# A two-layer encoder on one core: two groups of small products spread over four quadrants of TensorE, new durations in a list schedule, and two groups of loads on another queue

## The chip, the cores and the metric
The kernel runs on one core of a Trainium2 chip. The core has TensorE (PE in the rows, PEld for its weight loads), VectorE (DVE), ScalarE (ACT), GpSimd (POOL) and SyncE (SP), which here only issues transfers. The metric is the device time of one execution in microseconds. The kernel before took 4117.68 us, the median of three runs (4116.34 to 4122.85).

## The reference
The input x is 1024 positions of 1024 columns in float32. Two layers run one after the other, and each does this:

```
u  = x @ w_in                              # one input projection, cut into the columns of three branches
A  = rwkv7(u_A) * silu(z_A)                # 16 heads of 64, forwards and backwards over the positions
        state = state*w + (state@(-kk)) b^T + v k^T ;  y = state @ r
B  = pool(u_B) * silu(z_B)                 # means over windows 2, 4, 8, 16, minus itself, times a matrix
C  = attention(u_C) * silu(z_C)            # rotary positions, three (window, dilation) groups
m  = sum over branches of sigmoid(gate) * (branch @ proj)
x  = LayerNorm(alpha * x + m @ w_out)
```

All matrices that carry the model are float32, and the result is float32.

## The kernel before, in words
Dense products are made from split numbers: a float32 weight tile is cast to a rounded high part (ScalarE, L551), its low part is the difference (GpSimd or VectorE, L552), and each product is three matmuls of 128x128 by 128x512: L583 (high by high), L584 (low by high) and L585 (high by low). Such three are called a triple here. The class `Dense` issues them and prepares a weight piece one piece ahead.

A layer has five stages. In the rwkv stage (0 to some 1220 us in layer 0) the recurrence is done in chunks of 64 positions: per chunk a 64x64 triangular system per head is inverted in steps (`T`, `U`, `X`, with products at L1054 and casts at L1059), v's right sides are multiplied by the inverse (`av`, L1022, copied from PSUM to SBUF by ScalarE at L1025), the product for the state update follows (`nkt`, L1008, copied at L1012), and then each chunk goes through four steps in order: `A` multiplies the state by the chunk's rows (L1143 and L1146; VectorE adds at L1150), `W` scales the state (ScalarE, L1154), `B` multiplies the right sides by the inverse (L1161; ScalarE copies the result to `uv` at L1165), and `Cc` makes the outputs and the new state from them (L1175, L1180; VectorE, L1185). A step treats two heads and two directions at once, so `B` is four 64x64 products and `A` eight; `av` treats four chunks of each direction together, 16 products. A 64x64 product takes one quadrant of TensorE's array, which the halves of rows and columns (`HS[h]`) name; in float32 it is two matmul instructions. In the attention stage (1240 to 1600 us) VectorE rotates q and k in three operations (L1387, L1391, L1394), and the score products (L1447) need the result. The pool stage follows (to 1760 us), then the projections of branches C and B (to 1860 us: `ev_c`, L1741, and `ev_b`, L1752 and L1754, take the dense results off PSUM; meanwhile branch A's gated output is read back, L1772, cast to its high part by ScalarE, L1776, and split by GpSimd, L1778), and last the merge (to 2056 us: projection of A, output weights `wor` L1819, product L1842 to L1844, normalisation L1870 to L1883).

The order on every engine is set by the class `Sched`. Pieces of work, `Th`, say which engines they use and for how long (`("P", 230.0)` is 230 ns on TensorE; D, A, G, S are VectorE, ScalarE, GpSimd and SP), what they need and give, and which ring of PSUM buffers they hold ("m" for side work, two slots; "d" for dense). At each turn the list takes the piece that can start earliest by these numbers, and fills TensorE with dense triples in between. Each engine then runs its own instructions in that order; a waiting instruction stops those behind it on its engine.

Of the kernel before, what the change touches and what calls it, by code (L numbers as in the profile page):

```python
# [10 lines left out]
F32 = mybir.dt.float32  # L11
# [371 lines left out]
def trunk(ctx: ExitStack, tc: tile.TileContext, a: dict, out, dbg=None):  # L383
# [124 lines left out]
    class Dense:  # L508
# [56 lines left out]
        def make(self, src, nk, rhs, evac, halves=(0, 1), needs=(), gives=(), ev=(("A", 570.0),), key=None, ering=(), first=False):  # L565
# [62 lines left out]
    def rwkv(l):  # L628
        P = pc["P"]
        w_in = a["w_in"][l]  # L630
        with ExitStack() as es:
# [136 lines left out]
            def pair_kk(j):  # L768
# [76 lines left out]
                o.append(Th(f5, [("G", 3770.0)]))  # L845
# [151 lines left out]
            def joint(j, q):  # L997
# [28 lines left out]
                return ([Th(nkt, [("P", 930.0), ("A", 500.0), ("A", 500.0)], needs=[("sc", d, Q) for d in range(2)], ring=("m", "m"), gives=[("nkt", Q)])],  # L1026
                        [Th(av, [("P", 930.0), ("A", 500.0)], needs=[("nt", Q), ("uv" if q in (1, 2) else "uv0", j)], ring=("m",), gives=[("av", Q)])])
# [95 lines left out]
            def seq(j, q):  # L1123
# [4 lines left out]
                def step(i):  # L1128
# [6 lines left out]
                    def A():  # L1135
# [831 lines left out]
```

## Time and profile before

| | |
|---|---|
| median of three runs | 4117.68 us (4116.34 to 4122.85) |
| profiled execution | 4110.03 us, of which the span of the trace 4107.9 us |
| granted clock of TensorE, mean | 0.990 of full speed |
| TensorE (matmul) busy | 3933.5 us, 96% of the span |
| VectorE | 2344.7 us, 57% |
| ScalarE | 2224.0 us, 54% |
| GpSimd | 1653.9 us, 40% |

The span of the trace is the time from the first to the last instruction; the time of the execution has 2.1 us around it. A busy share is an average over stages with different loads; the rows below are read stage by stage. A bracket behind a row is the idle time of the engine ahead of it and what ended that.

### The profile page before, as it was taken

To read this page: it belongs to the slowest core of one execution; us is meant where nothing else is said; L and a number is where in the kernel's file an instruction comes from. 1 tells how busy PE (TensorE), PEld (TensorE's weight loads), DVE (VectorE), ACT (ScalarE), POOL (GpSimd) and SP (SyncE) were. 2 spreads that over 40 slices of the span, in tenths; PEclk is the share of its full clock that TensorE was granted. 3 is DMA by queue.
4 is the path that set the end of the run, shared out by engine and by line. 5 is a ranking of instruction groups with operands and counts; after the bars stand their busy time and mean duration, and the time that the engine had idled before them with its cause. 6 is when DMAs were issued, how large, how long until landed. Compare 5 with 4: busy or idle time off the path is not lost. (4 is left out here: it accounts for less than half of the span.)

```text
span 4107.9 us, 120670 instructions
## 1 busy us (share of the span) xinstructions
PE 3933.5 (96%) x51576; PEld 3060.1 (74%) x51576; DVE 2344.7 (57%) x4233; ACT 2224.0 (54%) x4390; POOL 1653.9 (40%) x2498
## 2 busy tenths in 40 slices
PE   8999999999999999999989999999999999999998
PEld 6677777777777788877767777777777777888777
DVE  3776766665533554545647667766665245454456
ACT  5677787777643442322146777777677434433210
POOL 4343444344433343453233444454434334334532
PEclk9999999999999999999999999999999999999999
DMA  2111111111114442155311111111111244421653
GB/s 90 32 48 43 44 42 45 45 42 44 58 58 119 130 134 91 54 181 192 123 51 30 48 40 44 42 48 40 43 47 54 76 114 133 127 83 55 191 182 116
DMA packets 329192, 326.41 MB, mean 79 GB/s; under 512 B 23536, under 2 KB 264384, under 8 KB 328655
## 3 DMA queue, kind: packets, MB, share of 16 engines
q1 hardware_dynamic: 301551, 233.66, 19.1%
q0 software_dynamic: 27104, 85.04, 5.9%
q8 instruction: 404, 6.62, 0.7%
q14 instruction: 133, 1.09, 0.1%
HBM read 224.86 MB, written 81.99 MB: 75 GB/s over the span
## 5 line engine op out<-in xcount | busy, mean ns | idle before, releaser
L583 PE MATMUL psdn<-xh,wh 128*128 128x512 f32 x3136 | 1331.1, 424 | 9.1 <-ACT wh L551 8.2
L585 PE MATMUL psdn<-xh,wl 128*128 128x512 f32 x3136 | 1240.8, 396 | 9.5 <-POOL wl L552 9.3
L584 PE MATMUL psdn<-xl,wh 128*128 128x512 f32 x3136 | 1236.5, 394 | 0.0
L552 POOL TENSOR_TENSOR wl<-wr,wh 128x512 fp32r<-128x512 f32 (+1 forms) x436 | 599.4, 1375 | 1313.1 <-ACT wh L551 1287.5
L583 PEld LDWEIGHTS psdn<-xh,wh 128*128 128x128 f32 x3136 | 594.5, 190 | 169.0 <-issue 31.0
L585 PEld LDWEIGHTS psdn<-xh,wl 128*128 128x128 f32 x3136 | 593.8, 189 | 151.4 <-POOL wl L552 19.5
L584 PEld LDWEIGHTS psdn<-xl,wh 128*128 128x128 f32 x3136 | 596.2, 190 | 101.0 <-issue 4.8
L551 ACT CAST wh<-wr 128x512 fp32r<-128x512 f32 (+2 forms) x484 | 290.3, 600 | 697.6 <-PE psdn L584 351.1
L1059 ACT CAST U<-pst 64x512 f16<-64x512 f32 x768 | 444.8, 579 | 116.9 <-PE pst L1054 100.1
L1087 DVE TENSOR_TENSOR X<-pst,c 128x512 f16<-128x512 f32 x320 | 219.4, 685 | 198.2 <-PE pst L1054 198.1
L1185 DVE SCALAR_TENSOR_TENSOR sbd<-sqp,wc,sbd 128x64 f32<-128x64 f32 x480 | 113.8, 278 | 216.9 <-PE sqp L1180 156.4
L1165 ACT COPY uv<-sqp 64x128 f32<-64x128 f32 x512 | 131.5, 257 | 85.0 <-PE sqp L1161 76.9
L1054 PEld LDWEIGHTS <-X 64*64 64x64 f16 x6144 | 144.1, 108 | 26.6 <-DVE sc L983 8.4
L1154 ACT ACTIVATE sbd<-sbd,wc 128x64 f32<-128x64 f32 x480 | 140.3, 340 | 43.1 <-PE sqp L1146 30.6
L1071 POOL TENSOR_TENSOR nl<-sc,nh 64x512 f16<-64x512 f32 x128 | 154.7, 1209 | 8.2 <-ACT nh L1068 3.0
L1054 PE MATMUL pst<-U,X 64*64 64x64 f16 x5120 | 153.6, 197 | 2.1 <-ACT U L1059 0.9
L1161 PEld LDWEIGHTS sqp<-u,sc 64*64 64x64 f32 x2048 | 80.1, 133 | 91.4 <-issue 50.2
L978 PE MATMUL pssc<-ar,nk 64*64 64x128 f32 x4096 | 146.4, 274 | 0.4
L1054 PEld LDWEIGHTS <-U 64*64 64x64 f16 x5120 | 113.1, 109 | 44.9 <-issue 14.5
L1054 PE MATMUL pst<-X,U 64*64 64x64 f16 x5120 | 140.3, 194 | 0.3
L1143 PEld LDWEIGHTS sqp<-sbd,ar 64*64 64x64 f32 x2048 | 83.6, 133 | 73.9 <-issue 43.7
L1150 DVE TENSOR_TENSOR u<-sqp,sc 128x128 f32<-128x128 f32 x256 | 73.4, 287 | 113.5 <-PE sqp L1146 61.0
(707 smaller groups left out, 7707.5 us busy)
## 6 DMA issues: line engine op xcount, KB each, us to landing
wr<-in_w_in_dram SPq DMA_DIRECT2D x360, 256.0 KB, 2.9
sga<-gt POOLq DMA_DIRECT2D x96, 256.0 KB, 2.3
g<-sga SPq DMA_DIRECT2D x96, 256.0 KB, 4.4
wr<-in_proj_a_dram SPq DMA_DIRECT2D x64, 256.0 KB, 3.0
sza<-sz POOLq DMA_DIRECT2D x32, 256.0 KB, 3.2
bva<-bv POOLq DMA_DIRECT2D x32, 256.0 KB, 2.5
oa<-o POOLq DMA_DIRECT2D x32, 256.0 KB, 3.0
oat<-oa SPq DMA_DIRECT2D x32, 256.0 KB, 3.6
```

Source lines behind the costliest of these rows:

```text
L551: nc.scalar.copy(hi[:, 0:n, :], r[:, 0:n, :])
L552: self.lo.tensor_tensor(out=lo[:, 0:n, :], in0=r[:, 0:n, :], in1=hi[:, 0:n, :], op=ALU.subtract)
L583: nc.tensor.matmul(ps, lhsT=hi[:, kk, :], rhs=ah, start=(k == 0), stop=False)
L584: nc.tensor.matmul(ps, lhsT=hi[:, kk, :], rhs=al, start=False, stop=False)
L585: nc.tensor.matmul(ps, lhsT=lo[:, kk, :], rhs=ah, start=False, stop=(k == nk - 1))
L978: nc.tensor.matmul(ps[h][HS[h if x == 0 else 1 - h], c, :], lhsT=nk[HS[h], c, x, :], rhs=ar[HS[h], c].rearrange("p a t -> p (a t)"), start ...
L1054: nc.tensor.matmul(ps[HS[1 - h if mir else h], d, c], lhsT=l, rhs=r, start=start and d == 0 and c == 0, stop=stop, skip_group_check=True)
L1059: nc.scalar.copy(dst[HS[h]], ps[HS[1 - h]])
L1071: nc.gpsimd.tensor_tensor(out=nl[HS[h]], in0=sc[HS[h], :, :, h, 0:64], in1=nh[HS[h]], op=ALU.subtract)
L1087: tt(out=x, in0=ps[0], in1=mask(i + 1), op=ALU.mult)
L1154: act(sbd[d], sbd[d], AF.Copy, scale=J["wc", d, Q % NB][:, pl[d][0]:pl[d][0] + 1])
L1165: nc.scalar.copy(uv[HS[h], two, h, :], pu[HS[h], 128:256].rearrange("p (s e) -> p s e", s=2))
```

## The change
It has four parts. In `av` the 32 instructions go to four quadrants of two PSUM tiles instead of two quadrants of one; the first direction's half is copied whole and the second's in two halves of the partitions, since two of its quadrants are the other way round; it holds both slots of ring "m" (one after its first copy). In `B` the eight instructions go to four quadrants, those of one row half in one of the step's two PSUM tiles and those of the other in the other, with four copies of 64x64 instead of two of 64x128; in `A` the rows for `py` are issued ahead of those for `pu`. The durations that the list uses are other numbers in many places (of which two stand in the diff; TensorE's own durations elsewhere stay). Branch A's read-back and the output weights are issued on SP instead of GpSimd. The first read-back waits for VectorE's last product of the pool branch, y times its gate, L1692 before and L1696 now.

```diff
-                    sc, ps = J["sc", Q], psm.tile([128, 2, 4, 64], F32, tag="m", name="psav")
+                    sc = J["sc", Q]
+                    ps = [psm.tile([128, 4, 64], F32, tag="m", name="psav") for _ in range(2)]
                     uv = J["uv", j, int(q in (1, 2))]
-                    for d in range(2):
-                        for i in range(4):
+                    for i in range(4):
+                        for d in range(2):
                             c, n, _ = place(d, q, i)
                             for h in range(2):
-                                nc.tensor.matmul(ps[HS[h], d, i], lhsT=sc[HS[1 - h], d, c, h, 0:64], rhs=uv[HS[1 - h], n, h, :],
+                                nc.tensor.matmul(ps[d][HS[h if d == 0 else 1 - h], i], lhsT=sc[HS[1 - h], d, c, h, 0:64], rhs=uv[HS[1 - h], n, h, :],
                                                  start=True, stop=True, skip_group_check=True)
                     yield
-                    nc.scalar.copy(sc[:, :, :, 1, 0:64], ps)
+                    nc.scalar.copy(sc[:, 0, :, 1, 0:64], ps[0])
+                    yield "first"
+                    for h in range(2):
+                        nc.scalar.copy(sc[HS[h], 1, :, 1, 0:64], ps[1][HS[1 - h]])
                 return ([Th(nkt, [("P", 930.0), ("A", 500.0), ("A", 500.0)], needs=[("sc", d, Q) for d in range(2)], ring=("m", "m"), gives=[("nkt", Q)])],
-                        [Th(av, [("P", 930.0), ("A", 500.0)], needs=[("nt", Q), ("uv" if q in (1, 2) else "uv0", j)], ring=("m",), gives=[("av", Q)])])
+                        [Th(av, [("P", 480.0), ("A", 280.0), ("A", 560.0)], needs=[("nt", Q), ("uv" if q in (1, 2) else "uv0", j)], ring=("m", "m"), gives=[("av", Q)])])
...
+                                nc.tensor.matmul(py[HS[1 - h], y0 + 64 * s:y0 + 64 * s + 64], lhsT=ar[HS[h], c, 1, :], rhs=sbd[d][HS[h]],
+                                                 start=d == 0, stop=False, skip_group_check=True)
+                            for h in range(2):
                                 nc.tensor.matmul(pu[HS[h], 64 * d:64 * d + 64], lhsT=ar[HS[h], c, 0, :], rhs=sbd[d][HS[h]],
                                                  start=d == 0, stop=True, skip_group_check=True)
-                            for h in range(2):
-                                nc.tensor.matmul(py[HS[1 - h], y0 + 64 * s:y0 + 64 * s + 64], lhsT=ar[HS[h], c, 1, :], rhs=sbd[d][HS[h]],
-                                                 start=d == 0, stop=False, skip_group_check=True)
...
-                        pu, uv = J["p"][1], J["uv", j, io]
+                        p, uv = J["p"][::-1], J["uv", j, io]
                         for d in range(2):
-                            c, n, s = pl[d]
                             for h in range(2):
-                                nc.tensor.matmul(pu[HS[h], 128 + 64 * s:192 + 64 * s], lhsT=J["sc", Q][HS[h], d, c, 0, 0:64], rhs=J["u0"][HS[h], d, :],
+                                nc.tensor.matmul(p[h][HS[d], 384:448], lhsT=J["sc", Q][HS[h], d, pl[d][0], 0, 0:64], rhs=J["u0"][HS[h], d, :],
                                                  start=False, stop=True, skip_group_check=True)
                         yield
                         for h in range(2):
-                            nc.scalar.copy(uv[HS[h], two, h, :], pu[HS[h], 128:256].rearrange("p (s e) -> p s e", s=2))
+                            for d in range(2):
+                                nc.scalar.copy(uv[HS[h], pl[d][1], h, :], p[h][HS[d], 384:448])
...
-                    return [Th(A, [("P", 230.0), ("D", 220.0)], needs=na, gives=[("read", j, n)]), Th(B, [("P", 240.0), ("A", 400.0)]),
+                    return [Th(A, [("P", 230.0), ("D", 220.0)], needs=na, gives=[("read", j, n)]), Th(B, [("P", 130.0), ("A", 780.0)]),
...
-                                       side=(("A", 307.0), ("G" if self.lo is nc.gpsimd else "D", 620.0 if self.lo is nc.gpsimd else 335.0)) if kk == 0 and h == halves[0] else (),
+                                       side=(("A", 520.0), ("G" if self.lo is nc.gpsimd else "D", 1235.0 if self.lo is nc.gpsimd else 602.0)) if kk == 0 and h == halves[0] else (),
...
-                    o += [Th(f0, [("S", 3000.0)], needs=[("raw", n, ct)]), Th(f1, [("D", 1160.0)]), Th(f2, [("D", 1160.0)]),
-                          Th(f3, [("D", 1160.0)], gives=[("rope", n, ct)])]
+                    o += [Th(f0, [("S", 3000.0)], needs=[("raw", n, ct)]), Th(f1, [("D", 1900.0)]), Th(f2, [("D", 2070.0)]),
+                          Th(f3, [("D", 1500.0)], gives=[("rope", n, ct)])]
...
-                    nc.gpsimd.dma_start(out=t, in_=oz[k * 128:(k + 1) * 128, hs])
+                    nc.sync.dma_start(out=t, in_=oz[k * 128:(k + 1) * 128, hs])
...
-                load.append(Th(fn, [("G", 1040.0)], lag=LDW, needs=[("oas", l, n - 6)] if n > 5 else (), gives=[("oal", l, n)], chain=False))
+                load.append(Th(fn, [("S", 100.0)], lag=LDW, needs=[("oas", l, n - 6)] if n > 5 else (), gives=[("oal", l, n)], chain=False))
...
-                    nc.gpsimd.dma_start(out=t, in_=a["w_out"][l][k * 128:(k + 1) * 128, :])
+                    nc.sync.dma_start(out=t, in_=a["w_out"][l][k * 128:(k + 1) * 128, :])
...
-                return [Th(load, [("G", 1040.0)], lag=3500.0, needs=[("pa", 0)] + ([("wo", k - 3)] if k > 2 else []), gives=[("wl", k)], chain=False)], \
+                return [Th(load, [("S", 100.0)], lag=3500.0, needs=[("pa", 0)] + ([("wo", k - 3)] if k > 2 else []), gives=[("wl", k)], chain=False)], \
```

How it moves instructions. On TensorE at the start of the rwkv stage, the difference of the orders ahead of the first product L823 (`psr`, which needs the normed `nx`), with + for what stands there now; psdn is the dense result, and these are the last three of four triples that are put there:

```order
+L583 MATMUL psdn<-xh,wh 128x512
+L584 MATMUL psdn<-xl,wh 128x512
+L585 MATMUL psdn<-xh,wl 128x512
+L583 MATMUL psdn<-xh,wh 128x512
+L584 MATMUL psdn<-xl,wh 128x512
+L585 MATMUL psdn<-xh,wl 128x512
+L583 MATMUL psdn<-xh,wh 128x512
+L584 MATMUL psdn<-xl,wh 128x512
+L585 MATMUL psdn<-xh,wl 128x512
 L823 MATMUL psr<-cst,nx 128x128 x4
```

The first product L823 thus has eight triples behind the second L781 instead of four; the same count holds in layer 1. In the attention of either layer, counted in dense triples of the whole program up to the product, the six products L1447 (L1451 now) that open an attention unit stand 4, 4, 4, 1, 4 and 1 triples later. The last L1246 of the rwkv stage has 18 triples between itself and the last `Cc` instead of 14.

On ScalarE at the head of the projections, before (y is the pool branch, wr a weight piece as loaded and wh its cast, ozt branch A's output as read back and xh its cast):

```order
L1689 ACTIVATE y<-psdn,pc 128x512 x2
L551 CAST wh<-wr 128x512
L551 CAST wh<-wr 128x256 x2
L1776 CAST xh<-ozt 128x512 x2
L551 CAST wh<-wr 128x512
L1776 CAST xh<-ozt 128x512
```

And the same place now:

```order
L1693 ACTIVATE y<-psdn,pc 128x512 x2
L1780 CAST xh<-ozt 128x512
L551 CAST wh<-wr 128x512
L1780 CAST xh<-ozt 128x512 x2
L551 CAST wh<-wr 128x256
L1780 CAST xh<-ozt 128x512 x3
L551 CAST wh<-wr 128x256
```

One cast of the read-back now stands between the last work on the pool branch and the cast of a weight piece of 128x512, and the casts of weights have one to three of them ahead of each.

On GpSimd at the same place, before (obl is the low part of the pool branch, m and t the sums of the projections, xl the low part of the read-back):

```order
L1694 TENSOR_TENSOR obl<-y,obh 128x512 x2
L1772 DMA ozt<-oz 128x512 x6
L1754 TENSOR_TENSOR m<-m,t 128x512
L1778 TENSOR_TENSOR xl<-ozt,xh 128x512
L1754 TENSOR_TENSOR m<-m,t 128x512
L1772 DMA ozt<-oz 128x512
L1778 TENSOR_TENSOR xl<-ozt,xh 128x512 x2
L1772 DMA ozt<-oz 128x512 x2
L1778 TENSOR_TENSOR xl<-ozt,xh 128x512 x2
```

And now:

```order
L1698 TENSOR_TENSOR obl<-y,obh 128x512 x2
L1782 TENSOR_TENSOR xl<-ozt,xh 128x512 x6
L1758 TENSOR_TENSOR m<-m,t 128x512 x2
L1782 TENSOR_TENSOR xl<-ozt,xh 128x512 x6
L1758 TENSOR_TENSOR m<-m,t 128x512 x2
L1782 TENSOR_TENSOR xl<-ozt,xh 128x512 x4
```

The loads of ozt are gone from this engine, and its subtractions for branch A stand in runs of six, six and four, with the sums of the projections between them.

## Rows read from the trace of the kernel before

**Rows 1.** Busy time of each engine in four stretches (columns in the first line).
```profile
core 0: us, PE busy (x) PEld busy (x) DVE busy (x) ACT busy (x) POOL busy (x), PEclk, DMA share, GB/s
200.00:1200.00 1000.00, 979.74 (x19863) 735.62 (x19858) 641.34 (x1345) 739.75 (x1537) 423.97 (x800) 1.00 0.15 46
...
1240.00:1600.00 360.00, 347.31 (x1872) 286.34 (x1871) 175.59 (x272) 141.96 (x264) 134.80 (x135) 0.99 0.43 125
1760.00:1860.00 100.00, 91.62 (x384) 72.61 (x383) 47.45 (x58) 20.14 (x40) 53.35 (x50) 0.98 0.63 200
1860.00:2056.00 196.00, 187.10 (x820) 148.69 (x820) 122.61 (x202) 37.59 (x61) 61.59 (x50) 0.98 0.47 155
```

**Rows 2.** TensorE's waits over the span: total us, times, longest us.
```profile
PE pssc L1447 <- DVE rawk L1394: 25.5, 12, 3.0
PE psdn L583 <- DVE m L1741: 16.3, 6, 5.2
PE sqp L1161 <- DVE u L1150: 14.4, 31, 1.7
PE psr L823 <- ACT nx L796: 12.1, 4, 5.9
PE psy L1246 <- POOL ysq L1241: 10.6, 8, 4.1
...
PE sqp L1175 <- ACT uv L1165: 0.7, 2, 0.4
```

**Rows 3.** Timeline: start us, length us, line, operation, count: a step's B.
```profile
439.18 0.45 PE L1161 MATMUL sqp<-u,sc 64*64 64x64 f32 x8
...
439.56 0.50 PE L583 MATMUL psdn<-xh,wh 128*128 128x512 f32 x1
```

**Rows 4.** Timeline: the inverse's product and the dense matmul behind it.
```profile
833.15 1.15 PE L1022 MATMUL psav<-uv,sc 64*64 64x64 f32 x32
...
834.23 0.51 PE L583 MATMUL psdn<-xh,wh 128*128 128x512 f32 x1
```

**Rows 5.** Timeline: the state update's product on four quadrants.
```profile
455.89 1.11 PE L1008 MATMUL psnt<-cst,nk 64*64 64x64 f32 x64
...
456.93 0.50 PE L583 MATMUL psdn<-xh,wh 128*128 128x512 f32 x1
```

**Rows 6.** ScalarE's copies by line: count, ns minimum, median and maximum.
```profile
L1165 ACT COPY uv<-sqp x512: 240/260/263, 157.7 to 3248.8; 64x128 f32<-64x128 f32 x171
...
L1025 ACT COPY sc<-psav x64: 562/586/598, 128.8 to 3209.8; 128x512 f32<-128x512 f32 x64
```

**Rows 7.** Timeline: first and last score product of layer 0, idle time in brackets.
```profile
1263.61 0.95 PE L1447 MATMUL pssc<-rawk,rawq 64*128 64x128 f32 x6 [2.95 <-DVE rawk L1394]
...
1508.83 0.49 PE L1447 MATMUL pssc<-rawk,rawq 64*128 64x256 f32 x2 [0.75 <-DVE rawk L1394]
```

**Rows 8.** Timeline: the head of the projections, layer 0.
```profile
1759.22 0.61 ACT L551 CAST wh<-wr 128x512 fp32r<-128x512 f32 x1
...
1761.07 0.69 DVE L1692 TENSOR_TENSOR y<-y,sz 128x512 f32<-128x512 f32 x1
...
1761.67 0.69 DVE L552 TENSOR_TENSOR wl<-wr,wh 128x512 fp32r<-128x512 f32 x1
...
1762.28 0.68 DVE L1741 SCALAR_TENSOR_TENSOR m<-g,psdn 128x512 f32<-128x512 f32 x1
...
1763.10 0.47 PE L583 MATMUL psdn<-obh,wh 128*128 128x512 f32 x1 [1.87 <-DVE m L1741]
```

**Rows 9.** Timeline: later in the same stage.
```profile
1799.04 7.08 DVE L552 TENSOR_TENSOR wl<-wr,wh 128x256 fp32r<-128x256 f32 x1 [0.91 <-ACT wh L551]
...
1802.13 3.70 POOL L1778 TENSOR_TENSOR xl<-ozt,xh 128x512 fp32r<-128x512 f32 x3
...
1806.77 0.79 PE L583 MATMUL psdn<-obh,wh 128*128 128x512 f32 x1 [5.17 <-DVE m L1741]
```

**Rows 10.** DMA issues: queue, count, KB each, median us from issue to landing.
```profile
oat<-oa SPq DMA_DIRECT2D x32, 256.0 KB, 3.6
```

More of the change, by code (lines that the diff above doesn't have):

```diff
@@ L844, in pair_kk @@
                           Th(f4(g), [("P", 428.0), ("D", 660.0)], ring=("m",), drop=hold[g])]
-                o.append(Th(f5, [("G", 3770.0)]))
+                o.append(Th(f5, [("G", 4300.0)]))
                 for g in range(2):
@@ L1409, in fn @@
                         nc.scalar.copy(vts[slot][:, g0:g0 + n, :, 0:64], ps[:, 0:n, :].rearrange("p n (h c) -> p n h c", h=2))
-                    o.append(Th(fn, [("P", 428.0), ("A", 478.0)], needs=([("raw", "v", ct)] + prev) if g0 == 0 else (), ring=("m",),
+                    o.append(Th(fn, [("P", 428.0), ("A", 588.0)], needs=([("raw", "v", ct)] + prev) if g0 == 0 else (), ring=("m",),
                                 gives=[("vt", ct)] if g0 + 4 >= len(offs) else ()))
@@ L1501, in t4 @@
                                                 in_=o_[64 * rr:64 * rr + 64])
-                return [Th(t2, [("D", 602.0), ("A", 800.0)], needs=[("t1", n)]), Th(t3, [("P", 428.0), ("A", 478.0)]),
+                return [Th(t2, [("D", 602.0), ("A", 800.0)], needs=[("t1", n)]), Th(t3, [("P", 428.0), ("A", 590.0)]),
                         Th(t4, [("P", 432.0), ("D", 200.0)], needs=[("vt", ct)] if first else (),
@@ L1545, in combine @@
                 nd = [("att", ct, h) for ct in range(2, 6) for h in range(2)] + [("attu", ct, h, t // 2) for ct in range(2) for h in range(2)]
-                return [Th(c1, [("S", 200.0)], needs=nd, gives=[("cl", t)], lag=4500.0), Th(c2, [("D", 300.0), ("A", 250.0)], needs=[("cl", t)]), Th(c3, [("D", 2600.0)]),
-                        Th(c4, [("P", 430.0), ("D", 330.0), ("A", 300.0), ("D", 300.0)], ring=("m",), needs=[("szc", 0), ("szc", 1)])]
+                return [Th(c1, [("S", 200.0)], needs=nd, gives=[("cl", t)], lag=4500.0), Th(c2, [("D", 300.0), ("A", 250.0)], needs=[("cl", t)]), Th(c3, [("D", 3100.0)]),
+                        Th(c4, [("P", 430.0), ("D", 418.0), ("A", 406.0), ("D", 476.0)], ring=("m",), needs=[("szc", 0), ("szc", 1)])]
             dense, ro, vt, un, cb = [], [Th(ld_c, [("S", 200.0)], needs=[("raw", "q", order[0])])], [], [[], []], []
@@ L1556, in attention @@
                     nd = prev if nm != "v" else ([("vt", order[n - 1])] if n >= 1 else [])
-                    dense += dn.tile(w_in[:, col * 128:(col + 1) * 128], 8, xr, qkv_evac(nm, ct, col, dil), needs=nd, gives=[("raw", nm, ct)], key=(col, l))
+                    dense += dn.tile(w_in[:, col * 128:(col + 1) * 128], 8, xr, qkv_evac(nm, ct, col, dil), ev=(("A", 1020.0),), needs=nd, gives=[("raw", nm, ct)], key=(col, l))
                 ro += rope(ct, dil)
@@ L1564, in attention @@
                 col = ZC // 128 + i
-                dense += dn.tile(w_in[:, col * 128:(col + 1) * 128], 8, xr, szc_evac(i), gives=[("szc", i)], ev=(("A", 1140.0), ("D", 600.0)))
+                dense += dn.tile(w_in[:, col * 128:(col + 1) * 128], 8, xr, szc_evac(i), gives=[("szc", i)], ev=(("A", 1366.0), ("D", 700.0)))
             for i in range(24 - NGA, 24):
@@ L1645, in f3 @@
                     tt(out=ml, in0=w, in1=mh, op=ALU.subtract)
-                return [Th(f1, [("D", 1100.0)], needs=[("praw", i)] + ([("y", 2)] if i == 3 else [])), Th(f2, [("D", 1300.0 if i % 3 != 1 else 2400.0)]),
-                        Th(f3, [("D", 1080.0), ("A", 950.0), ("D", 1080.0)], gives=[("mix", i)])]
+                return [Th(f1, [("D", 2870.0)], needs=[("praw", i)] + ([("y", 2)] if i == 3 else [])), Th(f2, [("D", 1300.0 if i % 3 != 1 else 2400.0)]),
+                        Th(f3, [("D", 1285.0), ("A", 1050.0), ("D", 1225.0)], gives=[("mix", i)])]
             def wsrc(H, ot):
@@ L1763, in proj_bc @@
                 cs = slice(d * 128, (d + 1) * 128)
-                dense += dn.tile(a["proj_c"][l][:, cs], 2, rh(och, ocl), ev_c(d), ev=(("D", 600.0),), key=("c", l) if d == 0 else None)
-                dense += dn.tile(a["proj_b"][l][:, cs], 6, rh(obh, obl), ev_b(d), ev=(("D", 600.0), ("G", 1225.0)), key=("b", l) if d == 0 else None)
+                dense += dn.tile(a["proj_c"][l][:, cs], 2, rh(och, ocl), ev_c(d), ev=(("D", 686.0),), key=("c", l) if d == 0 else None)
+                dense += dn.tile(a["proj_b"][l][:, cs], 6, rh(obh, obl), ev_b(d), ev=(("D", 686.0), ("G", 1419.0)), key=("b", l) if d == 0 else None)
             load, split = [], []
@@ L1893, in token @@
                     for k in range(8):
-                        d.append(Th(mm(k, n), [("P", 640.0)] + ([("D", 1200.0)] if k == 7 else []), rows=1.0, chain=False,
+                        d.append(Th(mm(k, n), [("P", 640.0)] + ([("D", 1380.0)] if k == 7 else []), rows=1.0, chain=False,
                                     ring=("d",) if k == 0 else (), hold=hold if k < 7 else None, drop=hold if k == 7 else None,
@@ L1897, in token @@
                 o.append(Th(stat, [("D", 200.0), ("A", 100.0), ("D", 300.0)], needs=[("tok", t)]))
-                o.append(Th(norm, [("D", 1270.0), [("G", 1225.0), ("D", 1200.0)], ("S", 100.0)]))
+                o.append(Th(norm, [("D", 1985.0), [("G", 1627.0), ("D", 2344.0)], ("S", 100.0)]))
                 if not last:
-                    o += [Th(back(g), [("P", 428.0), ("A", 480.0), ("D", 602.0)], ring=("m",)) for g in range(2)]
+                    o += [Th(back(g), [("P", 428.0), ("A", 588.0), ("D", 684.0)], ring=("m",)) for g in range(2)]
                 return d, o
@@ L1905, in merge @@
                 for d in range(8):
-                    dense += dn.tile(a["proj_a"][l][:, d * 128:(d + 1) * 128], 8, xr, ev_a(d), halves=(h,), ev=(("D", 2200.0),),
+                    dense += dn.tile(a["proj_a"][l][:, d * 128:(d + 1) * 128], 8, xr, ev_a(d), halves=(h,), ev=(("D", 2950.0),),
                                      key=("a", d, l) if h == 0 else None, gives=[("pa", 8 * h + d)])
```

6 lines of the change are left out of this document (3 added, 3 removed).

## The prediction

> **What bounds the kernel now.** I read the page's first part, then the busy time by stage, then TensorE's waits, then the timeline around the places that the change touches. TensorE is busy for 3933.5 of 4107.9 us. In the rwkv stage of layer 0 it is busy 979.74 of 1000 us, and ScalarE, which gets the new copies, 739.75 [rows 1]. So in that stage, some 1200 us of each layer, time is saved only where TensorE's own work gets shorter. In the attention and the two late stages TensorE idles 12.7, 8.4 and 8.9 us per stretch, and there the order of the work decides. Its waits are listed one by one: 25.5 us for the rope's last add, 16.3 us for the VectorE product of the projections, 12.1 and 10.6 us at the start and the end of the rwkv stage [rows 2].
>
> **B in four quadrants.** Now four fp32 products, 8 matmul instructions, go to two quadrants, four to each; TensorE starts its next dense matmul 0.38 us after the first of them (439.18 to 439.56) [rows 3]. The inverse's product puts 32 on two quadrants, 16 to each, and the next dense matmul comes 1.08 us after the first [rows 4]. From both, one instruction holds its quadrant for (1.08 - 0.38) / (16 - 4) = 0.058 us. That quadrants run beside each other is seen where 64 instructions go to all four, again 16 to each: 455.89 to 456.93, 1.04 us [rows 5]. In the new form B has 2 per quadrant and saves 2 x 0.058 = 0.117 us. There are 256 of them, since ScalarE's 512 copies of it come two to a step [rows 6]: 29.9 us.
>
> **The inverse's product in four quadrants.** 8 per quadrant instead of 16 saves 8 x 0.058 = 0.467 us; 64 times, one for each of its copies [rows 6]: 29.9 us. Together 59.8 us gross. Full-array dense matmuls share nothing, but in the order before a small matmul of another step stands on at least one side of 232 of the 256 B's and of all 64 of the other product; where that one already used the free quadrants, the time is not there twice. I take 52 and bound it by 30 and 60. Step A keeps its 16 instructions on four quadrants and only swaps halves: nothing.
>
> **ScalarE pays.** A copy of 128 columns is 260 ns and one of 512 columns 586 [rows 6], which makes 0.85 ns a column, 206 ns for 64 columns and 368 for 256 (estimates from these two). B's copies become 4 x 206 = 824 instead of 520 ns, 304 more, 256 times: 78 us. The other product's copy of 586 ns becomes three of 256 columns, 3 x 368 = 1104, 518 more, 64 times: 33 us. So 111 us fall on an engine that is 74% busy there; it goes to about 79%. None of it need be on TensorE's path, since dense matmuls fill the wait for a copy, but the chain from one step to the next gets 0.3 us longer. TensorE waits 14.4 us in all for this recurrence's VectorE step now [rows 2]; I charge 10 us, between 0 and 111.
>
> The trace has ScalarE 26% idle in this stage. The Trainium skill, in "TensorEngine Tiling (Array Packing)", section "PSUM Bottleneck", says that after the speed-up by tiling the copy out of PSUM may become the bottleneck, and that copies should be made over several tiles of a bank at once; this change does the opposite, two copies become four. By that rule the whole 111 us could come back; by the row only what the 26% can't take in. I go by the row, and the other is a rival below.
>
> **The list's new durations.** They move matmuls. The first score product of the attention now stands behind four more dense triples than before, the second, third and fifth too, the fourth and sixth behind one more; a triple is 0.70 us (three matmuls of 0.235). Its twelve waits are eight of some 2.8 us and four of 0.76 [rows 2, 7]. Four triples cover 2.8, one covers 0.7: 2.8 + 2.7 + 2.8 + 0.7 + 0.76 + 0.7 = 10.4 a layer, 20.9 for both. The rope itself may end a little later for work put ahead of it on VectorE: I take 18, between 8 and 24. At the start of rwkv four more triples go ahead of the first product that waits for the normed activations, longest wait 5.9, and at its end four more ahead of the last group norm product, longest 4.1 [rows 2]: 2.8 each, in both layers 5.6 and 5.6; neither is more than its waits, 12.1 and 10.6.
>
> **The loads on SP.** In the head of the projections ScalarE's list has the first cast of branch A's reload ahead of the weight cast that TensorE needs four triples later. Before, that cast ran at 1759.22, long before it was needed, and the next product followed at 1763.10 after 1.87 us of waiting [rows 8]. Now the chain is: last product of the pool branch ends on VectorE at 1761.76 (the load waits for its buffer), 0.3 to issue, 3.6 to land (the nearest load on SP [rows 10]), reload's cast 0.61, weight cast 0.61, weight's low part 0.69, product 0.68, and 0.14 to TensorE: 1768.4. That is 5.3 us later than 1763.10. Behind the six reloads SP has the next weight load of the c projection and a gate's load; six issues of 0.4 us put them 2.4 us back, and what they bring is used tiles later: nothing. In return GpSimd loses its load issues and does its subtractions in one run of six. That is where the worst wait lies: a VectorE subtraction that takes 0.69 us at twice the size [rows 8] took 7.08 us while GpSimd worked (three subtractions in 3.70 us, so 1.2 each, lie wholly inside), and TensorE then waited 5.17 us [rows 9]. A run of six could hold VectorE again.
>
> The row shows VectorE held across three GpSimd subtractions and more. The Trainium skill, in "SBUF — State Buffer" (the rules on the shared port pair), says that a VectorE operation with two SBUF inputs and a GpSimd operation that reads SBUF exclude each other, and the later one waits for the first one to end. By that, one GpSimd subtraction of 1.2 us is the price and the head costs 6.5; by the row it is three or more, and the head costs 8.9 at least. Where they differ the row decides.
>
> So the head costs 5.3, or 6.5 with VectorE held for one subtraction of 1.2 us, or 12.5 if held to the end of six. I take 6.5, since GpSimd's six can't all be ready at once while the reloads land one after the other. The later waits of this kind are 16.3 / 2 - 1.87 = 6.3 us a layer [rows 2, 8]; I add one subtraction, 1.2. Sum 7.7 a layer, 15 for both; the bounds are -2 (the head covered after all, 1 us of the late waits gone) and +35 (12.5, and a second wait of 5.2). In the merge the output weights come by SP instead of GpSimd; all idle time of TensorE there is 8.9 us [rows 1], and with new durations in the order it may lose or gain that: 0, within 8 either way.
>
> **The sum.** -52 + 10 - 18 - 5.6 - 5.6 + 15.4 = -55.8. The profiled execution took 4110.0 us (its span of 4107.9 and 2.1 around it), 7.7 below the median of the runs, 4117.7. So 4054 for such an execution, and 4062 for the median.
>
> **Rivals.**
> First, the copies decide. For: ScalarE at 79%, its copies sit between two steps of a recurrence, and its list is in order, so a copy behind a long cast of a weight is late. Against: TensorE's next products wait for ScalarE's copies of B for 0.7 us in all now [rows 2]. With all 111 us on the path it is 4062 - 10 + 111 = 4163; slower than before from the point where more than 74 of the 111 reach TensorE.
> Second, the late stages starve. For: the cast behind a load, and the 7.08 us. With the bound of 35 there instead of 15, and 8 lost in the merge, 4062 + 20 + 8 = 4090; it decides if TensorE's wait in the head is over 10 us.
> Third, quadrants don't help: neighbours already fill them, or the dense matmuls wait for the same spans. Then -52 is gone and the rest is -4: 4114. Against: rows 5 show four quadrants at once.
> Fourth, everything goes well: the head is covered since dense work is found for it (-2 in place of +15), the full 60 are saved and the copies hidden. -60 - 21 - 11 - 2 = -94, less the merge's 8: 4016 to 4024, say 4020.
>
> **How the numbers follow.** The forecast has a chance of 0.56 (4040 to 4082), the copies 0.06, starving 0.20, no help from quadrants 0.07, all well 0.11. What a measurement can tell from no change is 0.2%, 8.2 us: below 4109.5 is faster. The forecast, the starving and the good case are faster but for a tail of the starving one (0.02); no help lies on both sides of the line, 0.02 faster and 0.05 the same. The copies slower, 0.06, and 0.01 of the starving tail. So faster 0.87, same 0.06, slower 0.07. The range leaves out the copies, no help, and the lower half of the good case: 4020 to 4103.
>
> **What would show it.** In the rwkv stage: TensorE's two products (8 and 32 instructions) in about 0.26 and 0.6 us alone, ScalarE at 78 to 80% busy, TensorE still at 97% or more, and 25 us less per layer to the end of the stage. Waits for the rope's add under 6 us in all. In the head, a wait of about 8 us on the weight's cast or the product where 1.87 stood. Wrong it would be if TensorE's waits for B's copies grew past 40 us, or if the head's wait stayed under 2 us, or if the two products' spans did not shrink.

## The result, and the profile after

The changed kernel took 4067.78 us (4061.39 to 4072.09, four runs) beside 4117.01 for the kernel before: a ratio of 0.9877, 95% interval 0.986 to 0.9894. 4062 was forecast. The total is close; the way to it is not the one that the prediction worked out. The profiled execution took 4061.39 us, the shortest of the four; that of before took 4110.03.

The page's first part, after:

```profile
span 4059.6 us, 121248 instructions
...
PE 3871.7 (95%) x51576; PEld 3001.1 (74%) x51576; DVE 2325.1 (57%) x4233; ACT 2337.2 (58%) x5030; POOL 1652.4 (41%) x2450
```

TensorE is busy 61.8 us less over the span. Busy time by stretch, after:

```profile
core 0: us, PE busy (x) PEld busy (x) DVE busy (x) ACT busy (x) POOL busy (x), PEclk, DMA share, GB/s
200.00:1200.00 1000.00, 955.89 (x19804) 709.96 (x19803) 641.79 (x1338) 786.56 (x1828) 430.00 (x803) 1.00 0.14 45
2200.00:3200.00 1000.00, 959.91 (x20014) 714.28 (x20006) 650.90 (x1351) 796.79 (x1842) 425.58 (x786) 1.00 0.14 45
1240.00:1600.00 360.00, 359.40 (x1939) 296.29 (x1938) 177.23 (x277) 145.17 (x270) 144.05 (x142) 1.00 0.42 124
```

In the rwkv stage TensorE now idles 44 and 40 us in 1000 where it idled 20 [rows 1]; in the attention it hardly idles. Its waits over the span, after (total us, times, longest; `u` is VectorE's sum in step A, `uv` what the copies of B write, `y` the outputs of a step):

```profile
PE sqp L1164 <- DVE u L1154: 17.0, 30, 1.4
PE psy L1250 <- POOL ysq L1245: 15.0, 12, 4.3
PE sqp L1179 <- ACT uv L1169: 14.3, 31, 0.9
PE psdn L583 <- DVE m L1745: 14.1, 2, 7.1
PE sqp L1147 <- DVE y L1196: 12.4, 22, 1.0
PE sqp L1147 <- DVE y L1194: 10.1, 21, 0.9
...
PE psr L823 <- ACT nx L796: 2.0, 2, 1.0
...
PE pssc L1451 <- DVE rawk L1398: 1.9, 4, 0.7
```

The rope's wait fell from 25.5 to 1.9 us and that for nx from 12.1 to 2.0 [rows 2]. In their place stand new waits in the recurrence: for the copies of B (L1179, 14.3 us, was 0.7) and for VectorE's read of y ahead of step A (22.5 us in two rows, not among the rows before). One step of B alone, and the inverse's product, after (start, length, line, count):

```profile
417.15 0.34 PE L1164 MATMUL sqp<-u,sc 64*64 64x64 f32 x8
417.43 0.50 PE L583 MATMUL psdn<-xh,wh 128*128 128x512 f32 x1
```

```profile
845.62 0.69 PE L1023 MATMUL psav<-uv,sc 64*64 64x64 f32 x32
846.24 0.50 PE L583 MATMUL psdn<-xh,wh 128*128 128x512 f32 x1
```

The next dense matmul comes 0.28 us after B's first instruction instead of 0.38 [rows 3] and 0.62 us after the other product's instead of 1.08 [rows 4]. Quadrants do run beside each other. The new copies by line (count, ns minimum, median, maximum):

```profile
L1169 ACT COPY uv<-sqp x1024: 186/207/211, 150.9 to 3219.8; 64x64 f32<-64x64 f32 x171
...
L1026 ACT COPY sc<-psav x64: 349/373/375, 132.3 to 3183.7; 128x256 f32<-128x256 f32 x64
...
L1029 ACT COPY sc<-psav x128: 364/368/371, 135.8 to 3184.5; 64x256 f32<-64x256 f32 x128
```

207 ns for 64 columns: the estimate was 206. The median copy thus has the length that was expected of it; how close the four of a step follow each other is taken up at the copies alone. And the head of the projections in layer 0, where the last product of the pool branch is L1696 and the read-back's cast L1780:

```profile
1735.50 1.73 POOL L1698 TENSOR_TENSOR obl<-y,obh 128x512 fp32r<-128x512 f32 x1 [1.43 <-DVE y L1696]
...
1736.18 1.60 DVE L1696 TENSOR_TENSOR y<-y,sz 128x512 f32<-128x512 f32 x1
...
1737.81 2.71 SPq L1776 DMA_DIRECT2D ozt<-oz  x6
...
1741.08 0.62 ACT L1780 CAST xh<-ozt 128x512 fp32r<-128x512 f32 x1 [5.74 <-DMA ozt<-oz]
1741.61 0.61 ACT L551 CAST wh<-wr 128x512 fp32r<-128x512 f32 x1
1741.78 5.62 POOL L1782 TENSOR_TENSOR xl<-ozt,xh 128x512 fp32r<-128x512 f32 x4 [2.66 <-ACT xh L1780]
...
1742.25 1.34 DVE L552 TENSOR_TENSOR wl<-wr,wh 128x512 fp32r<-128x512 f32 x1 [4.47 <-ACT wh L551]
1743.51 0.68 DVE L1745 SCALAR_TENSOR_TENSOR m<-g,psdn 128x512 f32<-128x512 f32 x1
...
1744.34 0.77 PE L583 MATMUL psdn<-obh,wh 128*128 128x512 f32 x1 [7.08 <-DVE m L1745]
```

The chain is the predicted one: product, six loads on SP, cast of the read-back, weight cast, its low part, product, TensorE. The wait is 7.08 us where it was 1.87 [rows 8].

To see where the time went, I divide each layer at five marks in the timeline: last group norm product, last score product, first matmul of the C projection, first and last of the B projection. Dense triples move across the marks, so a stretch is corrected by 0.70 us for each triple more or fewer in it than before (10 more in each rwkv stretch, 11 fewer in each pool stretch). These are single executions, so a difference of a few us between two kernels says little. Differences to the kernel before in us, both layers added:

| stretch | forecast | after |
|---|---|---|
| rwkv | -53.2 | -17.1 |
| attention | -18 | -29.1 |
| pool | 0 | -4.5 |
| head of the projections | +13 | +10.4 |
| rest of the projections | +2.4 | -13.6 |
| merge | 0 | +5.7 |
| span | -55.8 | -48.3 |

### The profile page after: what moved, and what is told of

It reads as the page before. It is cut to its first block, busy times and chain, and to the rows that moved or that the text cites. A ratio compares the mean times of both kernels' runs of the same rounds, so it can differ in the third digit from the quotient of the medians.

```text
span 4059.6 us, 121248 instructions
## 1 busy us (share of the span) xinstructions
PE 3871.7 (95%) x51576; PEld 3001.1 (74%) x51576; DVE 2325.1 (57%) x4233; ACT 2337.2 (58%) x5030; POOL 1652.4 (41%) x2450
## 5 line engine op out<-in xcount | busy, mean ns | idle before, releaser
L552 POOL TENSOR_TENSOR wl<-wr,wh 128x512 fp32r<-128x512 f32 (+1 forms) x436 | 608.5, 1396 | 1217.7 <-ACT wh L551 1151.1
L1169 ACT COPY uv<-sqp 64x64 f32<-64x64 f32 x1024 | 210.9, 206 | 71.0 <-PE sqp L1164 59.6
L624 POOL DMA_DIRECT2D sga<-gt x96 | 54.1, 563 | 239.0 <-ACT gt L623 176.1
L1058 PE MATMUL pst<-U,X 64*64 64x64 f16 x5120 | 143.7, 195 | 4.0 <-ACT U L1063 2.2
L964 POOL TENSOR_TENSOR nk<-ta,k 128x256 f32<-128x256 f32 x128 | 104.5, 820 | 88.1 <-ACT ta L957 85.8
```

Source lines behind the costliest of these rows:

```text
L552: self.lo.tensor_tensor(out=lo[:, 0:n, :], in0=r[:, 0:n, :], in1=hi[:, 0:n, :], op=ALU.subtract)
L1058: nc.tensor.matmul(ps[HS[1 - h if mir else h], d, c], lhsT=l, rhs=r, start=start and d == 0 and c == 0, stop=stop, skip_group_check=True)
L1169: nc.scalar.copy(uv[HS[h], pl[d][1], h, :], p[h][HS[d], 384:448])
```

## The experiments

All compare with the kernel before on the same chip; the ratio's 95% interval stands in brackets. "Quadrants" are the inverse's product, A and B with their copies and their own numbers; "numbers" are all the list's other durations and the loads on SP. Code lines are shortened at `...`. Where two changed kernels are compared, it is by their medians; where their intervals meet, that is said.

**Quadrants alone.** The kernel before with this edit (and the same in `av` and `A`):

```diff
+nc.tensor.matmul(p[h][HS[d], 384:448], ...)
+Th(av, [("P", 480.0), ("A", 280.0), ("A", 560.0)], ...)
+Th(B, [("P", 130.0), ("A", 780.0)])
```

> The kernel before with the rwkv part of the change alone: the inverse's product and B in four quadrants, their copies, py ahead of pu, their durations in the list; late stages and loads as before. In the changed kernel TensorE's matmuls in these products got 53 us shorter, but the end of the rwkv stages, counted with the dense triples done by then, came only some 17 us earlier. Theory 1 (the gain is eaten inside the stage, by the longer copies and by py's wait): 4100 us, 15 to 20 faster than before, with 35 us more of TensorE waiting in the stage. Rival (the gain is eaten by the new durations of the list, which put other work in the way): 4072 us, 45 faster, and no more waiting in the rwkv stage than before.

Measured: 4148.59 us, 1.0078 (1.0061 to 1.0095). Slower by 32 us; neither account had that. The rwkv stretches are 18 and 21 us longer, not shorter. TensorE's waits:

```profile
PE sqp L1164 <- DVE u L1154: 31.2, 38, 3.2
...
PE sqp L1179 <- ACT uv L1169: 20.6, 30, 1.9
PE sqp L1147 <- DVE y L1196: 18.3, 20, 2.3
```

They are longer than in the changed kernel, that for u by 14 us. A part of the loss is the clock: TensorE had been granted full speed up to this wait. One wait, and the granted clock (third column from the end) behind it:

```profile
304.94 0.34 PE L1164 MATMUL sqp<-u,sc 64*64 64x64 f32 x8 [3.18 <-DVE u L1154]
```

```profile
300.00:310.00 10.00, 5.63 (x58) 3.79 (x58) 7.70 (x9) 4.33 (x12) 5.86 (x6) 0.80 0.31 92
310.00:320.00 10.00, 10.00 (x220) 7.93 (x221) 3.79 (x11) 7.54 (x19) 0.51 (x1) 0.86 0.01 3
```

Summed over the two stages, TensorE is granted half the clock (1.2 instead of 2.4 GHz) for some 27 us in each. By that, an estimate, it loses some 14 of these 18 and 21 us. In the kernel before it is none and 3 us.

**Numbers alone.**

```diff
-side=(("A", 307.0), ("G" ..., 620.0 ... else 335.0))
+side=(("A", 520.0), ("G" ..., 1235.0 ... else 602.0))
...
-nc.gpsimd.dma_start(out=t, in_=oz[...])
+nc.sync.dma_start(out=t, in_=oz[...])
...
```

The rope's durations and the output weights' loads go with them, as in the section on the change.

> The kernel before with the other part alone: the list's durations outside the quadrants and the loads on SP. Theory 1: this brings the larger part, 4085 us (32 faster): waits for the rope's last add down from 25 to 2 us, the start of rwkv 12 to 2. Rival: it brings little or costs, 4115 us or more, since the rwkv stage gets worse by it.

Measured: 4078.23 us, 0.9906 (0.9892 to 0.9921). So 39 of the 49 us are the numbers', 7 more than theory 1 had. TensorE's wait for nx fell to 2.1 us as it said, that for the rope only to 7.5. The attention stretches are 17 us shorter in this kernel, the rwkv stretches 11. The two parts don't add: with the old numbers quadrants cost 32 us, with the new ones they bring some 10 (4078 to 4068; the intervals just meet).

**The copies alone, under the old numbers.** B's products as before, its copies cut:

```diff
-nc.scalar.copy(uv[HS[h], two, h, :], pu[HS[h], 128:256]...)
+for d in range(2):
+    s_ = pl[d][2]
+    nc.scalar.copy(uv[HS[h], pl[d][1], h, :], pu[HS[h], 128 + 64 * s_:192 + 64 * s_])
...
-Th(B, [("P", 240.0), ("A", 400.0)])
+Th(B, [("P", 240.0), ("A", 780.0)])
```

> The kernel before with B's copies alone cut from two of 64x128 to four of 64x64 (and 780 instead of 400 ns in the list); products and quadrants as before. ScalarE gets 78 us more work. Theory 1 (the longer copy chain reaches TensorE): 14 to 25 us slower, 4135 us, with TensorE waiting 10 us or more on uv, where it waited 0.7 us. Rival (dense matmuls cover the copies): within 4 us of before, 4117 us.

Measured: 4159.72 us, 1.0105 (1.0085 to 1.0125), 43 us slower; neither account had that. The loss does not show as waits for uv, which stay at 0.8 us, but at u (17.7 us, was 14.4), at the state (14.9, was 6.8) and in the clock (31 us at half speed in the two rwkv stages, where it was 3). The edit changes the list's number for B as well, so copies and order are not apart here.

Nor are these the copies of the changed kernel. ScalarE's busy time rose by 28 us (2224.0 to 2252.5), not by 78. The first row is four copies of a step here, the second four of the changed kernel:

```profile
1030.31 0.64 ACT L1167 COPY uv<-sqp 64x64 f32<-64x64 f32 x4
```

```profile
998.54 0.85 ACT L1169 COPY uv<-sqp 64x64 f32<-64x64 f32 x4
```

A single one lasts 0.21 us in both. Here the second copy of a row half starts 0.11 us after the first, so that they overlap; in the changed kernel each starts 0.22 us after the one before it. The medians over all steps are 0.64 and 0.86 us for four, and 0.54 for the two copies of before. So this run gives the price of a shorter set of copies than the change has.

**A's halves swapped alone.**

```diff
+nc.tensor.matmul(py[HS[1 - h], ...], lhsT=ar[HS[h], c, 1, :], ...)
+for h in range(2):
 nc.tensor.matmul(pu[HS[h], ...], lhsT=ar[HS[h], c, 0, :], ...)
-for h in range(2):
-    nc.tensor.matmul(py[HS[1 - h], ...], lhsT=ar[HS[h], c, 1, :], ...)
```

> The kernel before with step A's halves swapped alone, py's products ahead of pu's. Theory 1 (py has to wait for VectorE's read of the step before, and now nothing is issued ahead of it): 8 to 12 us slower, 4127 us, with 20 us of TensorE waiting for y in front of A. Rival (these waits are the copies' delay seen elsewhere): within 3 us of before.

Measured: 4114.33 us, 0.9999 (0.9989 to 1.0008). TensorE waits 17.8 us for y, and the time is the same. The wait for the state in the same place (6.8 us before) is gone; what makes good the rest is not shown. The rival holds for the time. The reverse (the changed kernel with pu first) was not tried.

**One line of the numbers put back in the changed kernel.**

```diff
-side=(("A", 520.0), ("G" ..., 1235.0 ... else 602.0))
+side=(("A", 307.0), ("G" ..., 620.0 ... else 335.0))
```

> The changed kernel with one line of the numbers put back: the durations that the list takes for the splitting of a dense weight piece (ScalarE 307 instead of 520 ns, GpSimd 620 instead of 1235, VectorE 335 instead of 602). The quadrants alone made the kernel 32 us slower, with the numbers 10 us faster than the numbers alone. Theory 2 (the list must know that ScalarE is busy: with the low split costs it packs the recurrence's copies behind weight casts, and TensorE waits): most of the loss comes back in the rwkv stages, some 20 us each, 4105 us. Rival (other numbers of the list or chance of the order): 4068 us, rwkv stages as in the changed kernel within 5 us.

Measured: 4096.22 us, 0.9957 (0.994 to 0.9973), 28 us slower than the changed kernel. The rwkv stretches lose 19 and 20 us to it (17 and 20 us at half clock, where the changed kernel has none and 3), and the merge wins 4 and 6. This is what theory 2 had. The list places every side piece by what it believes of ScalarE, GpSimd and VectorE. With 307 ns for a cast that the trace has at 0.61 us [rows 8] it believed that ScalarE had room for the longer copies. The line holds three durations, and that ScalarE's is the one that counts was not tried.

**The changed kernel without B's quadrants.**

```diff
-nc.tensor.matmul(p[h][HS[d], 384:448], ...)
+nc.tensor.matmul(pu[HS[h], 128 + 64 * s:192 + 64 * s], ...)
...
-nc.scalar.copy(uv[HS[h], pl[d][1], h, :], p[h][HS[d], 384:448])
+nc.scalar.copy(uv[HS[h], two, h, :], pu[HS[h], 128:256]...)
...
-Th(B, [("P", 130.0), ("A", 780.0)])
+Th(B, [("P", 240.0), ("A", 400.0)])
```

Step A has pu first again.

> The changed kernel with step A and B, B's copies and their durations as before; the inverse's product stays in four quadrants. TensorE gets B's 27 us back, ScalarE loses 78 us of copies. Theory 1 (B's four copies cost in the recurrence about what its quadrants save): 4062 to 4072 us, no slower than the changed kernel. Rival (B's quadrants save their 27 us net): 4090 us or more.

Measured: 4056.29 us, 0.9857 (0.9842 to 0.9872), 11 us under the changed kernel (8 by the two ratios, whose intervals meet; every run of this one is faster than every run of that one). That is below what either account had: B's part of the change, its copies and A's order with it, costs some 10 us net. The waits in this kernel's recurrence, smaller than in the changed one:

```profile
PE sqp L1165 <- DVE u L1154: 11.7, 32, 1.8
...
PE sqp L1179 <- ACT uv L1169: 4.0, 12, 0.6
...
PE sqp L1147 <- DVE sbd L1189: 2.5, 6, 0.5
```

Against the numbers alone (4078), the inverse's quadrants bring 22 of the 24 us by which its matmuls' busy time fell.

**The changed kernel without the inverse's quadrants.**

```diff
-ps = [psm.tile([128, 4, 64], F32, tag="m", name="psav") for _ in range(2)]
+sc, ps = J["sc", Q], psm.tile([128, 2, 4, 64], F32, tag="m", name="psav")
...
-Th(av, [("P", 480.0), ("A", 280.0), ("A", 560.0)], ..., ring=("m", "m"), ...)
+Th(av, [("P", 930.0), ("A", 500.0)], ..., ring=("m",), ...)
```

> The changed kernel with the inverse's product on two quadrants and copied at once, as before; B stays in four. TensorE gets 26 us back, ScalarE loses 33 us. This product is off the recurrence, so its longer copy should be covered. Theory 1: its quadrants save most of their 26 us, so this kernel is 15 to 25 us slower than the changed one, 4088 us. Rival (it gains nothing either): 4068 us.

Measured: 4068.8 us, 0.9885 (0.9871 to 0.99): as the changed kernel within the intervals. So this product's quadrants bring 22 us without B's and nothing beside them. Theory 1 fails as stated; the two together bring no more than B's alone. Why they don't add is not shown.

**Half of B's copies on VectorE.**

```diff
-nc.scalar.copy(uv[...], ...)
+(nc.scalar.copy if h == 0 else nc.vector.tensor_copy)(uv[...], ...)
...
-("A", 780.0)
+[("A", 390.0), ("D", 390.0)]
```

> The changed kernel with two of B's four copies on VectorE and two on ScalarE (in the list 390 ns on each instead of 780 on ScalarE). The chain of a step gets some 0.4 us shorter and ScalarE loses 105 us / 2. Theory 1 (the copies' length in the chain is what ate B's gain): 4045 to 4055 us, waits for uv under 8 us. Rival (any small operation more between the steps costs, on whichever engine, or VectorE's queue is longer): 4068 us or more.

Measured: 4075.36 us, 0.9904 (0.9889 to 0.9918), 7 us slower than the changed kernel (the intervals meet); it is not faster. The waits for uv grew, and it is VectorE that ends them now:

```profile
PE sqp L1164 <- DVE u L1154: 23.6, 52, 1.5
PE sqp L1179 <- DVE uv L1169: 21.0, 34, 2.2
```

The test missed its aim. From the start of a step's first copy to the end of its last it still takes 0.87 us (median; 0.86 in the changed kernel), since in 189 of the 256 steps one engine's pair starts more than 0.1 us after the other's. So whether a shorter chain would bring B's gain back stays open. In the profiled execution TensorE is also at half clock for 18 and 14 us of the two rwkv stages, where the changed kernel has none and 3; by that, an estimate, it loses some 14 us.

**The head mended, B as before.** In the list the first six read-backs now need the pool branch's last output.

```diff
-needs=[("oas", l, n - 6)] if n > 5 else ()
+needs=[("oas", l, n - 6)] if n > 5 else [("y", 5)]
```

> The kernel with B as before and all the rest changed (4056 us when run), and in the list the first six read-backs of branch A need the pool branch's last output, so their casts stand behind the weight casts that TensorE needs. In the changed kernel and in that one the head of the projections is 5.2 us longer per layer, with one wait of 7 us. Theory (the cast ahead of the weight cast makes that wait): the head gets back to 4.8 us, 10 us in all: 4046 us. Rival (the work is late in any case, and the wait moves into the rest of the stage): 4056 us, head shorter and the rest of the stage longer by 5 a layer.

Measured: 4044.81 us, 0.9828 (0.9813 to 0.9842), the fastest of all, 23 us under the changed kernel, and as the theory had it. The head is 4.8 us again in both layers, and the rest of the stage is no longer than it was. The same place in this kernel:

```profile
1733.03 0.41 ACT L551 CAST wh<-wr 128x256 fp32r<-128x256 f32 x1 [1.25 <-PE psdn L584]
...
1734.24 0.67 DVE L1745 SCALAR_TENSOR_TENSOR m<-g,psdn 128x512 f32<-128x512 f32 x1
...
1734.76 2.36 SPq L1776 DMA_DIRECT2D ozt<-oz  x5
...
1735.06 0.47 PE L583 MATMUL psdn<-obh,wh 128*128 128x512 f32 x1 [1.87 <-DVE m L1745]
```

The product starts before the loads are issued, no cast of theirs stands ahead of it, and TensorE waits 1.87 us as in the kernel before [rows 8].

**The copies alone, under the new numbers.** The kernel without B's quadrants (4056), its copies cut in four.

```diff
-nc.scalar.copy(uv[HS[h], two, h, :], pu[HS[h], 128:256]...)
+nc.scalar.copy(uv[HS[h], pl[d][1], h, :], pu[HS[h], 128 + 64 * s_:192 + 64 * s_])
...
-Th(B, [("P", 240.0), ("A", 400.0)])
+Th(B, [("P", 240.0), ("A", 780.0)])
```

> The same kernel (B on two quadrants, 4056 us when run) with B's copies alone cut in four, under the new numbers: the price of the copies without the quadrants' gain. With both, the changed kernel, it was 4068. Theory (B's quadrants save about their 27 us and the copies cost more, about 38): 4085 to 4097 us. Rival (the quadrants save little, 10 us or less, since dense work fills them, and the copies cost about 11 to 20): 4066 to 4078 us.

Measured: 4070.74 us, 0.989 (0.9875 to 0.9905). The copies, with the list's number for them, cost 14 us here (43 under the old numbers). The rival holds for the time. Its reason, that the quadrants' 27 us are saved and not used, is not shown. The copies are again the shorter set of 0.64 us a step. ScalarE is busy 2288.5 us, with two copies 2255.1 and in the changed kernel 2337.2. So the changed kernel has the 27 us of TensorE's matmuls less than this one and 49 us of ScalarE's busy time more, and both together come out 3 us faster, inside the intervals. From B's first matmul to the end of its last copy it takes 1.28 us with two copies, 1.33 here and 1.46 in the changed kernel (medians).

```profile
PE sqp L1165 <- DVE u L1154: 19.4, 38, 2.0
...
PE sqp L1147 <- DVE sbd L1191: 7.9, 12, 1.3
```

Step A's wait for the state here (7.9 us) is smaller than that for y in the changed kernel, and waits for uv are 0.8.

**The loads on GpSimd again.**

```diff
-nc.sync.dma_start(out=t, in_=oz[...])
+nc.gpsimd.dma_start(out=t, in_=oz[...])
...
-load.append(Th(fn, [("S", 100.0)], ...))
+load.append(Th(fn, [("G", 1040.0)], ...))
...
```

The same two lines of the output weights go with them.

> The changed kernel with branch A's read-back and the output weights issued on GpSimd again, also in the list. Theory: the head loses its 7 us wait (5.2 a layer won), and the waits that VectorE's late subtractions and products made in the rest of the stage come back (7 us a layer lost), the merge gives back 2 to 4: 4063 to 4075 us, within 7 of the changed kernel. Rival (the loads on SP are what shortened the late stages): 4085 us.

Measured: 4066.46 us, 0.9879 (0.9863 to 0.9896): no change. The head loses its 5.2 us per layer as expected. But the rest of the projections stays 6.5 us shorter, so that gain is the numbers', not the queue's; the merge is 4 us a layer longer. The move of the loads gives and takes about the same.

**The list told that A waits for y.**

```diff
-Th(Cc, [("P", 470.0), ("D", 390.0, 200.0)]
+Th(Cc, [("P", 470.0), ("D", 590.0)]
```

> The changed kernel with one number of the list: after step Cc the next step A may start when VectorE has also read y, ("D", 590) instead of ("D", 390, and 200 more that A need not wait for). With py's products first, A does wait for that read, 22.5 us in all, which the old number does not tell the list. Theory (the list puts A too early, and knowing better it puts dense matmuls there): waits for y under 8 us, 4050 to 4060 us. Rival (the recurrence's chain is as long as it is, and the wait moves on to u and uv or to the end of the stage): 4063 to 4075 us.

Measured: 4069.32 us, 0.9887 (0.987 to 0.9903): no gain, as the rival had it. TensorE's waits for y:

```profile
PE sqp L1147 <- DVE y L1194: 17.5, 22, 3.6
...
PE sqp L1147 <- DVE y L1196: 8.3, 8, 2.0
```

25.8 us in place of 22.5, fewer and longer. One number for one step did not take the wait away. In the profiled execution TensorE is at half clock for 20 and 7 us of the rwkv stages, where the changed kernel has none and 3; by that, an estimate, it loses some 12 us. What the new order would be worth without these pauses is not shown.

## Why the prediction was right, and where it was not

The time was right through terms that were wrong in both directions: rwkv came out 36 us short of its forecast, and the attention, the pool and the rest of the projections 32 us better than theirs. That the total was within 6 us is luck.

- **Quadrants, TensorE's work: right.** 0.117 and 0.467 us a piece were worked out; the alone-standing pieces show 0.103 and 0.453. The matmuls' busy time fell by 26.8 us for B and 26.0 for the inverse, 52.8 in all, where I took 52.
- **The step that failed: "None of it need be on TensorE's path, since dense matmuls fill the wait for a copy", charged with 10 us.** The whole rwkv term was -53 and measured -17, and the numbers alone already have -11 there. What the runs show in its place: B in quadrants with its longer copies costs some 10 us net, where 27 us of its matmuls were saved. Four copies without quadrants, a shorter set, cost 14 us under the new numbers and 43 under the old. The waits for B's copies went from 0.7 to 14.3 us. Dense work did not fill these waits, though the list put 10 more triples into each rwkv stretch. TensorE is 96% busy there and still not alone in setting the pace. Whether it is the length of the copies, ScalarE's load or the order that the list makes of them is not shown and stays open. The two experiments on VectorE and on y leave it so, since the first did not shorten the chain and in both TensorE loses some of its clock.
- **The first rival, the copies, was part of it.** It needed 74 of 111 us on the path to turn the sign. Under the old numbers, quadrants and copies alone did turn it (32 us slower). The new numbers saved it, and these I had priced only for the waits that I could see move.
- **The list's numbers: the rope right, the rest not.** With the numbers alone the rope's wait lost 18.0 us and the attention stretches 17, where 18 was forecast. In the changed kernel they lost 23.6 and 29; why the quadrants, which do nothing in that stage, go with 12 more there is not shown. The wait for nx lost 10.1, not 5.6. At the end of the rwkv stage nothing was won: that wait went from 10.6 to 15.0 us, its longest from 4.1 to 4.3. And the line of split costs, which I passed over, is worth 28 us with the quadrants in.
- **The head: right within 1.3 us a layer.** 5.3 us later, or 6.5 with VectorE held for one subtraction, which I took: measured 5.2 in either layer. VectorE was held, and the read-back's cast came 3.3 us after the load was issued, not 3.9. VectorE's product took 1.60 us beside a GpSimd subtraction and the weight's low part 1.34, both where 0.69 was before. The Trainium skill, "SBUF — State Buffer" (the rules on the shared port pair), has the later of the two wait for the end of one; the rows agree here: the product begun at 1736.18 ends at 1737.78, 0.55 us behind the end of the subtraction at 1737.23. The 7.08 us of before [rows 9] is not explained by that. VectorE stood there beside five subtractions, not three; the other two are these, and a load's issue lies between:

```profile
1799.07 2.55 POOL L1778 TENSOR_TENSOR xl<-ozt,xh 128x512 fp32r<-128x512 f32 x2
```

- **The rest of the projections: wrong sign.** I expected 1.2 us more a layer from bunched subtractions; it got 6.8 less. The late waits for m [rows 2, 9] are gone, with the loads on either queue, so the new numbers did it.
- **The merge** cost 5.7 us, within the 8 given.
- **The signs.** The two products' spans, ScalarE's 79 to 80% and the waits for the rope came as said. TensorE is at 96% in the rwkv stage, not 97 or more, and the end of that stage came 8 us earlier a layer, not 25.

The Trainium skill, "TensorEngine Tiling (Array Packing)", section "PSUM Bottleneck", was the warning to weigh more: for B, tiling together with the copies out of PSUM that it asked for came out slower than neither (4068 us against 4056). Its other advice there, to use VectorE too, did not help as tried here (4075 us against 4068); the two engines' copies ran beside each other in a quarter of the steps.

## What to carry to other kernels

Where a written order fills the engines, time saved on the busiest engine need not come off the whole: put the list's numbers right first, and measure such an edit under them. Run the parts of an edit apart even when the whole is faster; here the kernel without one of them, with one need added in the list, is 23 us better. When a part is replaced by a stand-in, read its rows before the price is believed: the copies alone were not as long as those that they stood for. Where a load is moved, read off what its consumer now stands ahead of in the queues: that term could be worked out to about a microsecond.

## What was not expected of the hardware

In this kernel pauses were paid for twice. Behind a wait of 3.18 us in the quadrants-alone kernel TensorE was granted 0.80 and 0.86 of its clock over two stretches of 10 us, which is 2.0 + 1.4 = 3.4 us of full speed lost behind the wait of 3.2. Over the two rwkv stages there were some 27 us at half clock in each, against none and 3 before; that is some 14 of the 18 to 21 us by which each stage was longer (an estimate, as if TensorE alone set the time).

Two copies on ScalarE in a row can overlap or not. With B on two quadrants the two 64x64 copies of a row half, which read the same half of the partitions, start 0.11 us apart and last 0.21 each. In the changed kernel each copy reads the other half from the one before it, and they start 0.22 us apart. That the halves are the reason is not shown; the changed kernel's copies in another order were not tried.
